# Split projection weights stored once in DRAM scratch and loaded ready in the later rounds

## The chip, the core and the metric

The kernel runs on one core of a Trainium2 chip. The metric is the device time of one execution in microseconds, the median over the runs shown. The core has five engines that run side by side and wait for each other by semaphores: TensorE (PE; its weight loads are shown as PEld), VectorE (DVE), ScalarE (ACT), GpSimd (POOL) and SyncE (SP). SP computes nothing here; it issues nearly all DMAs, strictly in the order of its queue.

## What is computed

One layer of a decoder with two parallel groups of heads, over a prompt of 2048 rows and 8 x 8 sample rows with a paged cache:

```python
h = rmsnorm(x, norm_g)
z = h @ w_in                                   # 1024 -> 3656
q, k, v, qi, ki, wi, ga, u, vm, gm = jnp.split(z, offs, axis=-1)
...
score = indexer_scores(qib, wb, ki)            # causal, 8 index heads
idx, valid = select_keys(score, posb, k_top)   # 256 keys per query
o = sparse_attend(qb, take(k, idx), take(v, idx), valid)
...
mix = concat([attn_o * silu(ga), gelu(u) * s * silu(gm)])
r = x + mix @ w_out
return r + sigmoid(rmsnorm(r, ple_norm_g) @ w_ple_gate) * (p @ w_ple_proj)
```

The case turns on `h @ w_in`, with `w_in` of 1024 x 3656 fp32 values.

## The kernel before

The kernel has three phases. Phase A projects all rows, computes index scores, finds each query's 256 keys and multiplies the gated part by its half of `w_out`. Phase B is attention, phase C the output projection and the gate.

Precision beyond one fp32r matmul is had by splitting: a matrix is written as a high part, rounded to fp32r, and a low part, the rest. `proj` (L290) multiplies high by high, high by low and low by high into one PSUM tile `z`, 24 matmuls for a block of 128 rows and a chunk of columns.

The 17 blocks of rows (16 of the prompt, and SB with the sample rows) are handled in three rounds of 6, 6 and 5 blocks (`ROUNDS`, L55; SB is in the first). In every round all 14 column chunks of `w_in` (`CH`, L57) are loaded again: chunk x1 has 328 columns, the others 256. Chunk x1 holds the index key, x2 the second half of the index queries; then follow vm, k, v, u, gm, q and ga.

`load_w` (L261) fetches a chunk and splits it, in eight steps k of 128 rows. A step loads a raw tile (L270, three buffers), rounds it to the high part `whi` (L275, on POOL; in the very first chunk every other one on ACT, L273) and subtracts to get the low part `wlo` (L276). `WLO_DVE = [6, 5, 0]` says how many of the eight subtractions a round gives to DVE; the rest are POOL's. `whi` and `wlo` have two buffers each. The chunk after the running one is loaded while the running one is multiplied, so its split can start once the last matmul of the chunk before the running one has released the buffer.

After `proj`, `post` (L330) finishes each block: norms, rotary products and activations on ACT, DVE and POOL, and stores of small tiles (`qn`, three buffers; `vt`, two buffers) into DRAM scratch or outputs. `norm_h` (L232) and `split_h` (L246) prepare the rows of the next round during the last chunk of a round: a load of `x` (L226, two buffers), a square on ACT (L241), two small POOL steps (L242, L243), a scaling on DVE (L244), eight transposes on TensorE (L254), and a split on ACT and DVE (L123, L124).

Between the blocks `pump` (L435) advances two other chains: index scores (`idx`, L636: dots on TensorE at L661 and L662, ReLU on ACT at L664, weighted sum on DVE at L666; the sum starts from a ramp that POOL writes at L652) and the search for the 256th score (`topk`, L774: one ACT pass at L802 and a dozen small DVE instructions, seven times, then selections on DVE).

The order on each engine isn't that of the code. The program is built with a scheduler that works from a simulated timeline and places each instruction in its engine's queue. When the instructions change, the order of all engines changes.

Of the kernel before, what the change touches and what calls it, by code (L numbers as in the profile page):

```python
# [9 lines left out]
F32 = mybir.dt.float32  # L10
# [46 lines left out]
CH = [  # L57
    ("x1", [(1536, 72), (1024, 256)]),
    ("x2", [(1280, 256)]),
    ("vm0", [(2632, 256)]),  # L60
    ("vm1", [(2888, 256)]),
    ("k", [(512, 256)]),
    ("v", [(768, 256)]),
    ("u0", [(2120, 256)]),
    ("u1", [(2376, 256)]),
# [45 lines left out]
class Builder:  # L111
# [80 lines left out]
    def phase_a(self, eb):  # L192
        tc, nc, I, O = self.tc, self.nc, self.I, self.O
        with ExitStack() as es:
# [51 lines left out]
            def split_h(b):  # L246
# [3 lines left out]
                for j in range(2):  # L250
# [7 lines left out]
                    else:  # L258
                        self.split(hh[:, s], hl[:, s], ps)

            def load_w(ci, r):  # L261
                name, segs = CH[ci]
                n = sum(s[1] for s in segs)
                wh = wp.tile([128, 8, 328], F32R, name="whi")
                wl = wp.tile([128, 8, 328], F32R, name="wlo")
                for k in range(8):
                    raw = rp.tile([128, 328], F32, name="raw")
                    o = 0
                    for c0, cn in segs:
                        nc.sync.dma_start(raw[:, o:o + cn], I["w_in"][0, k * 128:(k + 1) * 128, c0:c0 + cn])  # L270
                        o += cn
                    if r == 0 and ci == 0 and k % 2:
                        nc.scalar.activation(wh[:, k, :n], raw[:, :n], AF.Copy)  # L273
                    else:
                        nc.gpsimd.tensor_scalar(wh[:, k, :n], raw[:, :n], 1.0, 1.0, op0=OP.mult, op1=OP.mult)  # L275
                    (nc.vector if k < WLO_DVE[r] else nc.gpsimd).tensor_tensor(wl[:, k, :n], raw[:, :n], wh[:, k, :n].bitcast(F32), OP.subtract)  # L276
                return wh, wl, n

            def load_out(j):
# [179 lines left out]
            gb = ac.tile([128, D], F32, name="gb")  # L459
            nc.sync.dma_start(gb, bcast(I["norm_in_g"], D))  # L460
            W0 = load_w(0, 0)
            norm_h(ROUNDS[0][0])
            split_h(ROUNDS[0][0])
# [27 lines left out]
            for si, (r, c) in enumerate(seq):  # L491
                blocks = ROUNDS[r]
                name = CH[c][0]
                nb = ROUNDS[r + 1] if r + 1 < len(ROUNDS) else []
                if name == "vm0":
                    t = vp.tile([128, 6, 512], F32, name="vn")
                    for j, b in enumerate(blocks):
                        vslot[b] = (t, j)
                if si == 1:
                    self.gmlp_weights(ac)  # L500
                nxt = load_w(seq[si + 1][1], seq[si + 1][0]) if si + 1 < len(seq) else None
                if not nxt:
                    ws = [load_out(0)]
# [1045 lines left out]
```

## Time and profile before

| | |
|---|---|
| three runs | 1964.53, 1956.28 and 1952.77 us, median 1956.28 |
| profiled execution, span from the first to the last instruction | 1952.4 us (the page gives no other time for it) |
| TensorE busy | 1865.8 us, 96% |
| DVE, ACT, POOL busy | 67%, 51%, 43% |
| DMA | 202.26 MB, 104 GB/s in the mean |
| HBM | 142.47 MB read, 57.42 MB written |

How to read it. A busy share is the time in which an engine executes at least one instruction; TensorE's matmuls overlap each other, so a busy TensorE is not one at its peak. A wait is idle time of an engine just before an instruction, put down to what released it last. The granted clock of TensorE is a share of its full speed. "DMA share" is the mean busy share of the core's 16 DMA engines. Phase A ends near 1084 us (last matmul of L552), phase B near 1590 us (last of L1128).

### The profile page before, as it was taken

The page shows a single profiled execution, that of the slowest core. Times are in us where ns is not written, and L with a number is a line of the kernel's source. Part 1 is how long each engine was busy: PE and PEld are TensorE (multiplying, and loading weights), DVE is VectorE, ACT ScalarE, POOL GpSimd, SP SyncE. Part 2 cuts the span into 40 slices and gives each one's busy share as a digit, 9 for nine tenths or more (in the row PEclk, how much of TensorE's full clock was granted, in tenths as well). Part 3 has the DMA queues.
Part 4 walks back from the last instruction along what each step waited for, and adds up shares of the span by engine and source line. Part 5 has one row for each costly group of instructions (what it writes and reads, how often), then busy time and mean ns, then how long its engine had stood idle before and what let it go on. Part 6 is the DMA issues. An engine that isn't in the chain of part 4 may idle for free. (4 is left out here: it accounts for less than half of the span.)

```text
span 1952.4 us, 35414 instructions
## 1 busy us (share of the span) xinstructions
PE 1865.8 (96%) x12370; PEld 1655.2 (85%) x12370; DVE 1317.3 (67%) x3682; ACT 995.7 (51%) x1907; POOL 830.4 (43%) x1323
## 2 busy tenths in 40 slices
PE   6989999899999899998999899999999999999998
PEld 5989989897998898997999778887788877888887
DVE  5496566488889758889752688888878865333321
ACT  3234325245555535665664788777867753122211
POOL 5482565554335679547513452213211155222311
PEclk9999999899999999998999999999999999999999
DMA  6423324423333432433455442222222064222311
GB/s 197 112 68 91 113 86 140 125 57 101 85 102 103 144 100 76 126 96 100 135 187 173 142 125 81 81 72 85 64 70 60 27 212 148 90 99 74 116 37 44
DMA packets 193687, 202.26 MB, mean 104 GB/s; under 512 B 85528, under 2 KB 160864, under 8 KB 193376
## 3 DMA queue, kind: packets, MB, share of 16 engines
q1 hardware_dynamic: 187872, 181.08, 30.9%
q0 software_dynamic: 5632, 18.88, 3.1%
q8 instruction: 98, 1.61, 0.4%
q14 instruction: 85, 0.70, 0.1%
HBM read 142.47 MB, written 57.42 MB: 102 GB/s over the span
## 5 line engine op out<-in xcount | busy, mean ns | idle before, releaser
L303 PE MATMUL z<-whi,hhi 128*128 128x256 f32 (+1 forms) x1792 | 461.3, 291 | 14.2 <-ACT qn L376 4.2
L304 PE MATMUL z<-wlo,hhi 128*128 128x256 f32 (+1 forms) x1792 | 455.0, 287 | 2.4 <-POOL wlo L276 2.4
L303 PEld LDWEIGHTS z<-whi,hhi 128*128 128x128 f32 x1792 | 342.7, 191 | 26.7 <-ACT qn L376 6.7
L304 PEld LDWEIGHTS z<-wlo,hhi 128*128 128x128 f32 x1792 | 342.7, 191 | 6.5 <-POOL wlo L276 2.7
L306 PE MATMUL z<-whi,hlo 128*128 128x256 f32 (+1 forms) x1792 | 269.6, 287 | 0.0
L275 POOL TENSOR_SCALAR whi<-raw 128x256 fp32r<-128x256 f32 (+1 forms) x332 | 151.2, 466 | 265.0 <-PE z L306 115.7
L306 PEld LDWEIGHTS z<-whi,hlo 128*128 128x128 f32 x1792 | 240.1, 189 | 4.8
L666 DVE SCALAR_TENSOR_TENSOR big<-dots,sgn,big 128x1024 f32<-128x1024 f32 (+7 forms) x176 | 178.7, 1016 | 43.3 <-ACT dots L664 42.6
L664 ACT ACTIVATE dots<-dots 128x1024 f32<-128x1024 f32 (+7 forms) x176 | 140.5, 801 | 118.4 <-PE dots L662 115.2
L124 DVE TENSOR_TENSOR b_pt<-b_tp,b_pt 128x512 fp32r<-128x512 f32 (+1 forms) x288 | 183.4, 656 | 14.1 <-ACT b_pt L123 12.0
L802 ACT ACTIVATE bfw<-big,tk 128x384 bf16<-128x384 f32 (+14 forms) x105 | 136.6, 1301 | 93.5 <-DVE tk L822 58.7
L123 ACT ACTIVATE b_pt<-b_tp 128x512 fp32r<-128x512 f32 (+1 forms) x288 | 156.1, 579 | 54.2 <-PE b_tp L1111 51.3
L1128 PE MATMUL b_o<-b_pt,Vst 128*128 128x512 f32 x544 | 182.9, 422 | 0.6 <-DVE b_pt L124 0.5
L1085 ACT ACTIVATE b_sm<-b_sm,b_st 128x128 f32<-128x128 f32 (+15 forms) x128 | 155.2, 1214 | 34.7 <-DVE b_st L1078 33.5
L1111 PE MATMUL b_tp<-mats,b_sm 128*128 128x128 f32 x1088 | 171.7, 274 | 0.3 <-ACT b_sm L1085 0.2
L1111 PEld LDWEIGHTS b_tp<-mats,b_sm 128*128 128x128 f32 x1088 | 132.2, 141 | 30.0 <-ACT b_sm L1085 2.0
L276 POOL TENSOR_TENSOR wlo<-raw,whi 128x256 fp32r<-128x256 f32 (+1 forms) x182 | 144.5, 803 | 6.2
L1076 PE MATMUL b_s<-Kst,b_qh 128*128 128x512 f32 (+3 forms) x320 | 139.8, 439 | 6.7 <-DVE b_st L1078 4.8
L1078 DVE CUSTOM_DVE_ANT_0 b_sm<-b_s,b_mask,b_st 128x512 f32<-128x512 f32 (+3 forms) x192 | 124.0, 646 | 23.9 <-PE b_s L1077 19.9
L661 PE MATMUL dots<-ki_stack,qih 128*128 128x512 f32 (+3 forms) x304 | 113.6, 376 | 10.7 <-DVE big L666 10.7
L1077 PE MATMUL b_s<-Kst,b_ql 128*128 128x512 f32 (+3 forms) x320 | 117.9, 371 | 0.1
L662 PE MATMUL dots<-ki_stack,qil 128*128 128x512 f32 (+3 forms) x304 | 111.9, 378 | 0.0
(344 smaller groups left out, 4095.4 us busy)
## 6 DMA issues: line engine op xcount, KB each, us to landing
raw<-w_in SPq DMA_DIRECT2D x336, 128.0 KB
x<-x_prompt SPq DMA_DIRECT2D x16, 512.0 KB
b_qr<-s_q SPq DMA_DIRECT2D x32, 256.0 KB
s_r<-hlo SPq DMA_DIRECT2D x32, 256.0 KB
c_r<-s_r SPq DMA_DIRECT2D x16, 512.0 KB
c_x<-x_prompt SPq DMA_DIRECT2D x16, 512.0 KB
y_prompt<-c_rn SPq DMA_DIRECT2D x15, 512.0 KB
qid<-s_qi SPq DMA_DIRECT2D x56, 128.0 KB
```

Source lines behind the costliest of these rows:

```text
L123: nc.scalar.activation(hi, src, AF.Copy)
L124: nc.vector.tensor_tensor(lo, src, hi.bitcast(F32), OP.subtract)
L275: nc.gpsimd.tensor_scalar(wh[:, k, :n], raw[:, :n], 1.0, 1.0, op0=OP.mult, op1=OP.mult)
L276: (nc.vector if k < WLO_DVE[r] else nc.gpsimd).tensor_tensor(wl[:, k, :n], raw[:, :n], wh[:, k, :n].bitcast(F32), OP.subtract)
L303: nc.tensor.matmul(z, lhsT=hh[:, k], rhs=wh[:, k, :n], start=(k == 0), stop=False)
L304: nc.tensor.matmul(z, lhsT=hh[:, k], rhs=wl[:, k, :n], start=False, stop=False)
L306: nc.tensor.matmul(z, lhsT=hl[:, k], rhs=wh[:, k, :n], start=False, stop=(k == 7))
L664: nc.scalar.activation(r, r, AF.Relu)
L666: nc.vector.scalar_tensor_tensor(a, r, self.sgn[:, b, h:h + 1], a, op0=OP.mult, op1=OP.add)
L1085: nc.scalar.activation(part, part, AF.Exp, bias=stt[:, h, c:c + 1], scale=-1.0, accum_out=stt[:, h, 4 + e:5 + e])
L1111: nc.tensor.transpose(ps[:, k, r], sm2[r][:, (k0 + k) * 128:(k0 + k) * 128 + 128], ident)
L1128: nc.tensor.matmul(o.rearrange("p a b -> p (a b)"), lhsT=Vst[:, kb, g].rearrange("p a d -> p (a d)"), rhs=pt[:, k].rearrange("p a b -> p ( ...
```

## The change

`load_w` gets a second way. Two DRAM scratch tiles per chunk, `s_wh` and `s_wl`, hold the chunk's high and low parts. In round 0 a chunk is loaded and split as before, and then both parts are stored, one DMA each. In rounds 1 and 2 nothing is split: four DMAs bring the two parts, each in two halves of four steps k, straight into `whi` and `wlo`.

```diff
+            kept = [tuple(self.dram.tile([128, 8, sum(s[1] for s in segs)], F32, name=f"s_w{e}{ci}") for e in "hl")
+                    for ci, (_, segs) in enumerate(CH)]
+
             def load_w(ci, r):
                 name, segs = CH[ci]
                 n = sum(s[1] for s in segs)
                 wh = wp.tile([128, 8, 328], F32R, name="whi")
                 wl = wp.tile([128, 8, 328], F32R, name="wlo")
+                halves = tuple(zip((wh, wl), kept[ci]))
+                if r:
+                    for k in range(0, 8, 4):
+                        for t, d in halves:
+                            nc.sync.dma_start(t[:, k:k + 4, :n].bitcast(F32), d[:, k:k + 4])
+                    return wh, wl, n
                 for k in range(8):
...
                     (nc.vector if k < WLO_DVE[r] else nc.gpsimd).tensor_tensor(wl[:, k, :n], raw[:, :n], wh[:, k, :n].bitcast(F32), OP.subtract)
+                for t, d in halves:
+                    nc.sync.dma_start(d, t[:, :, :n].bitcast(F32))
                 return wh, wl, n
```

Lines behind the insertions have numbers that are 9 to 11 higher in the changed kernel (L275 becomes L284, L276 L285, L365 L376); its ready loads stand at L273 and its stores at L287.

The first place is SP's queue at the start, while chunk x1 of round 0 is split. `x` is a block of rows, loaded for blocks 3 and 4 here and at the end for the sample rows; `raw` is a step of weights, `big` a small table. Before:

```order
L226 DMA x_336<-x_prompt 128x1024
L270 DMA raw_440<-w_in 128x256
L609 DMA big_762<-w_s 8x8x8 x6
L226 DMA x_359<-x_prompt 128x1024
L609 DMA big_762<-w_s 8x8x8 x2
L270 DMA raw_444<-w_in 128x256
...
L226 DMA x_382<-x_sample 64x1024
```

And now:

```order
L226 DMA x_366<-x_prompt 128x1024
L279 DMA raw_470<-w_in 128x256
L620 DMA big_794<-w_s 8x8x8 x5
L287 DMA s_wh0_221<-whi_253 128x2624
L226 DMA x_389<-x_prompt 128x1024
L620 DMA big_794<-w_s 8x8x8 x2
L279 DMA raw_474<-w_in 128x256
L620 DMA big_794<-w_s 8x8x8
L287 DMA s_wl0_222<-wlo_254 128x2624
...
L226 DMA x_412<-x_sample 64x1024
```

The store of the high part stands directly ahead of the load of block 4, and that of the low part between it and the load of the sample rows.

The second place is POOL's queue at the step from round 0 to round 1, where the rows of round 1 are normed. `hst` is the statistics tile of a block's norm (L242 and L243), `whi` and `wlo` are the weights of the next chunk, `qn` and `rope_t` a rotary product, `big` the ramp that starts an index sum. Before:

```order
L276 TENSOR_TENSOR wlo_4644<-raw_4665,whi_4643 128x256
L652 TENSOR_SCALAR big_5317<-iota_413 128x768
L242 TENSOR_SCALAR hst_4558<-hst_4558 128x1
L275 TENSOR_SCALAR whi_4643<-raw_4673 128x256
L276 TENSOR_TENSOR wlo_4644<-raw_4669,whi_4643 128x256
L134 TENSOR_TENSOR qn_4712<-qn_4712,ropet_288 128x4x16
L243 TENSOR_TENSOR hst_4558<-hst_4558,half_218 128x1
L276 TENSOR_TENSOR wlo_4644<-raw_4673,whi_4643 128x256
```

And now:

```order
L663 TENSOR_SCALAR big_5253<-iota_443 128x768
L242 TENSOR_SCALAR hst_4516<-hst_4516 128x1
L243 TENSOR_TENSOR hst_4516<-hst_4516,half_218 128x1
L242 TENSOR_SCALAR hst_4578<-hst_4578 128x1
L243 TENSOR_TENSOR hst_4578<-hst_4578,half_218 128x1
L663 TENSOR_SCALAR big_5512<-iota_443 128x896
```

The two steps of one block now stand side by side, and those of the next block follow directly.

The third place is SP's queue in round 1, where chunk x1 is multiplied. `kin` is an index key and `qn` an index query on their way to DRAM. Before, raw loads of chunk vm0 stand between them:

```order
L345 DMA idx_k_prompt<-kin_4927 128x64
L365 DMA s_qi9_77<-qn_4935 128x256
L270 DMA raw_5004<-w_in 128x256
L270 DMA raw_5008<-w_in 128x256
L365 DMA s_qi10_78<-qn_4982 128x256
L345 DMA idx_k_prompt<-kin_4974 128x64
L270 DMA raw_5012<-w_in 128x256
```

And now:

```order
L356 DMA idx_k_prompt<-kin_4919 128x64
L273 DMA wlo_4983<-s_wl2_226 128x4x256
L376 DMA s_qi9_77<-qn_4927 128x256
L273 DMA wlo_4983<-s_wl2_226 128x4x256
L273 DMA whi_4982<-s_wh2_225 128x4x256 x2
L356 DMA idx_k_prompt<-kin_4966 128x64
L376 DMA s_qi10_78<-qn_4974 128x256
```

Four ready loads of 512 KB stand where raw loads of 128 KB stood, and the index queries of blocks 9 and 10 have moved among and behind them.

## Rows read from the trace of the kernel before

**Rows 1.** The page, span and busy time of the engines.

```profile
span 1952.4 us, 35414 instructions
PE 1865.8 (96%) x12370; PEld 1655.2 (85%) x12370; DVE 1317.3 (67%) x3682; ACT 995.7 (51%) x1907; POOL 830.4 (43%) x1323
```

**Rows 2.** Busy time by stretch, rounds 0, 1 and 2; its first line names the columns.

```profile
core 0: us, PE busy (x) PEld busy (x) DVE busy (x) ACT busy (x) POOL busy (x), PEclk, DMA share, GB/s
0.00:324.00 324.00, 298.77 (x2206) 276.23 (x2207) 208.42 (x724) 122.77 (x291) 176.85 (x314) 0.99 0.40 114
324.00:663.00 339.00, 318.58 (x2377) 305.00 (x2378) 267.26 (x867) 166.06 (x316) 166.02 (x294) 0.97 0.36 102
663.00:965.00 302.00, 286.49 (x2062) 269.62 (x2061) 245.70 (x655) 177.11 (x276) 202.36 (x340) 0.98 0.36 104
```

**Rows 3.** Timeline of PE, first matmul of round 1: start us, us, instruction, count.

```profile
323.89 0.39 PE L303 MATMUL z<-whi,hhi 128*128 128x328 f32 x1
```

**Rows 4.** PE's waits in round 1: us in total, times, longest us.

```profile
PE tp L254 <- DVE hlo L124: 6.7, 2, 5.3
PE dots L661 <- DVE big L666: 3.1, 1, 3.1
...
PE tp L322 <- DVE qil L124: 2.3, 1, 2.3
...
PE z L303 <- POOL whi L275: 1.2, 1, 1.2
```

**Rows 5.** PE's waits in round 2.

```profile
PE dots L661 <- DVE big L666: 7.5, 3, 6.8
```

**Rows 6.** POOL's waits in round 0.

```profile
POOL whi L275 <- PE z L296: 46.9, 8, 13.1
```

**Rows 7.** Busy time by stretch, four spots where PE pauses; columns as in rows 2.

```profile
340.00:362.00 22.00, 14.24 (x78) 12.76 (x77) 12.95 (x37) 4.70 (x18) 9.01 (x22) 0.77 0.38 112
436.00:453.00 17.00, 11.61 (x66) 9.32 (x65) 14.94 (x69) 7.42 (x16) 14.75 (x20) 0.85 0.40 113
588.00:613.00 25.00, 20.50 (x140) 18.89 (x139) 24.36 (x74) 11.26 (x19) 15.71 (x24) 0.93 0.28 81
905.00:930.00 25.00, 16.86 (x98) 15.14 (x97) 23.71 (x73) 10.73 (x15) 19.45 (x28) 0.80 0.32 111
```

**Rows 8.** Busy time of L275 alone (POOL), rounds 1 and 2.

```profile
324.00:663.00 339.00, 51.71 (x115) 0.97 0.36 102
663.00:965.00 302.00, 45.74 (x102) 0.98 0.36 104
```

**Rows 9.** Busy time of L276 alone (DVE, then POOL), rounds 1 and 2.

```profile
324.00:663.00 339.00, 31.70 (x65) 39.62 (x47) 0.97 0.36 102
663.00:965.00 302.00, 0.00 (x0) 80.07 (x104) 0.98 0.36 104
```

**Rows 10.** Timeline of POOL at the step from round 0 to round 1.

```profile
336.25 0.19 POOL L242 TENSOR_SCALAR hst<-hst 128x1 f32<-128x1 f32 x1
336.52 1.55 POOL L275 TENSOR_SCALAR whi<-raw 128x256 fp32r<-128x256 f32 x1
338.04 0.73 POOL L276 TENSOR_TENSOR wlo<-raw,whi 128x256 fp32r<-128x256 f32 x1
...
339.02 0.55 POOL L243 TENSOR_TENSOR hst<-hst,half 128x1 f32<-128x1 f32 x1
```

**Rows 11.** Timeline of PE there; in brackets its idle time and the releaser.

```profile
347.79 1.97 PE L254 MATMUL tp<-mats,x 128*128 128x128 f32 x8 [5.28 <-DVE hlo L124]
```

**Rows 12.** Line L132, a rope product on DVE: count, duration ns min/median/max.

```profile
L132 DVE TENSOR_TENSOR rope_t<-qn,ropet x51: 175/185/1864, 128.0 to 935.3; 128x32 f32<-128x32 f32 x48, 64x32 f32<-64x32 f32 x3
```

**Rows 13.** Timeline of POOL in round 2.

```profile
913.04 1.90 POOL L652 TENSOR_SCALAR big<-iota 128x2048 f32<-128x2048 int16 x1
```

**Rows 14.** Timeline of SP at the start, the loads of x for block 4 and the sample.

```profile
24.52 0.36 SPq L226 DMA_DIRECT2D x<-x_prompt  x1
...
35.26 0.48 SPq L226 DMA_DIRECT2D x<-x_sample  x1
```

**Rows 15.** DVE's waits in round 2, the one for a store.

```profile
DVE qn L362 <- DMA s_qi<-qn: 1.5, 1, 1.5
```

## The prediction

> **What bounds the kernel now.** I read the busy shares first: the span is 1952.4 us and TensorE's matmuls are busy for 1865.8 of them, 96% [rows 1]. No other engine comes near, so an instruction taken from VectorE (DVE) or GpSimd (POOL) is worth nothing by itself. It is worth something only where TensorE waits behind it. Second I read the busy times by stage [rows 2]. The three rounds of the projection take 324, 339 and 302 us; a round begins where the 328-wide matmuls of chunk x1 return [rows 3]. In round 1 TensorE is idle 339 - 318.6 = 20.4 us, in round 2 302 - 286.5 = 15.5 us, and the granted clock is 0.97 and 0.98: 3% and 2% short, 10.2 and 6.0 us. The clock has two levels, 1.2 and 2.4 GHz, so these are stretches at the lower one, and the spots below show that they lie at TensorE's pauses. Together 52 us is all that rounds 1 and 2 can give back.
>
> Third I read who ended TensorE's pauses. In round 1 the longest are transposes of the next round's rows behind DVE (6.7 us), index dots behind DVE (3.1) and index queries behind DVE (2.3) [rows 4]; in round 2 index dots behind DVE (7.5) [rows 5]. The weights are hardly a cause: one wait for a high half is there, 1.2 us [rows 4], and GpSimd itself sits idle because the next weight buffer is still being read by matmuls, 46.9 us in eight places of round 0 [rows 6]. Weights come early. Fourth I looked for where the pauses lie: four spots hold 7.8 + 5.4 + 4.5 + 8.1 = 25.8 of the 35.9 idle us, with clocks of 0.77, 0.85, 0.93 and 0.80, which is 5.1 + 2.6 + 1.8 + 5.0 = 14.4 us short [rows 7]. In all four GpSimd is busy for 41 to 87% and DVE for 59 to 97%.
>
> **What goes.** The high halves (L275) take 51.7 us of GpSimd in round 1 and 45.7 in round 2 [rows 8]; the low halves (L276) take 31.7 us of DVE and 39.6 of GpSimd in round 1, and 80.1 of GpSimd in round 2 [rows 9]. All of it goes: 91 and 126 us of GpSimd, 32 us of DVE. It lies beside matmuls, so its direct worth is 0. What it gives at the four spots:
>
> - 340 to 362 us, the step from round 0 to round 1. The rows of the next round go DMA, ScalarE square, two GpSimd steps (L242, L243), DVE scale, TensorE transpose. GpSimd runs L242 at 336.25 and L243 only at 339.02, with a high half of 1.55 us and a low half between [rows 10]; the order shows both gone from there. The two steps take 0.19 and 0.55 us, so 339.02 - 336.44 = 2.6 us of pure queueing goes from one block and some more before L242. TensorE's pause before its last eight transposes is 5.28 us [rows 11]. I take 6 of the 7.8 idle us and 4 of the 5.1 clock us: 10.
> - 436 to 453 us: DVE is busy 14.9 of 17 us, low halves among it. I take 3 of 5.4 idle and 1.3 of 2.6 clock: 4.3.
> - 588 to 613 us: DVE is busy 24.4 of 25 us, mostly with the top-k search, which stays. I take 2 of 6.3.
> - 905 to 930 us, in round 2: no DVE instruction goes there, but GpSimd is busy 19.5 of 25 us. A DVE rope product that takes 185 ns in the median took 1864 ns once [rows 12], at 913 us, while GpSimd ran L652 for 1.90 us beside it [rows 13]. Instructions of the two engines hold each other up, so fewer on GpSimd also shortens DVE's. I take 2.7 of 8.1 idle and 1.7 of 5.0 clock: 4.4.
> - The 10 idle us outside the four spots: 2.
>
> The Trainium skill, page "SBUF — State Buffer", section "SBUF: two separate sides", states that DVE and GpSimd share one pair of ports under an exclusive lock, and the loser waits for the whole instruction. The trace agrees, with 1864 ns beside 1.90 us. Had DVE's instructions kept their length, the 905 us spot would give nothing, and the sum below would be 4.4 us smaller.
>
> Sum of the gains: 10 + 4.3 + 2 + 4.4 + 2 = 22.7, call it 23 us; bounds 0 (the pauses stay) and 52 (all go).
>
> **What comes.** Projection weights are 1024 x 3656 x 4 = 15.0 MB. Round 0 stores both halves, 30 MB more; rounds 1 and 2 read 30 MB in place of 15. The DMA rows give 102 GB/s at a share of 0.36 in round 1 [rows 2], so about 283 GB/s at a full share. A chunk of 2.1 MB then takes 7.4 us by this estimate, and the average chunk lasts 339 / 14 = 24 us and 302 / 14 = 22 us. Shares rise by 53 us of full transfer per later round: 0.36 + 53/339 = 0.52 and 0.36 + 53/302 = 0.54, and in round 0 by 106/324 to 0.73. Three prices:
>
> - The start. The order puts the store of chunk x1's high half ahead of the load of x for block 4, and that of its low half some rows later, ahead of the sample's x. Each is 1.34 MB, 4.7 us by the rate above. In the trace those loads issue at 24.52 and 35.26 us [rows 14]. The store waits for the last high half, whose split ends near 25 us, so block 4 is late by some 5 us; the matmuls of blocks 0 to 3 cover part. Bounds 0 and 9.4; I take 3.
> - The other stores of round 0. SP issues in order, so a store that waits for the splits holds what stands behind it (raw loads, index-query stores). The splits are early (46.9 us above), which is the cover. Were that cover gone, each of 13 chunks could lose a us. Bounds 0 and 13; I take 1.
> - The ready loads. They wait for the weight buffer, which the last matmul of the chunk before frees, so they can start when the running chunk starts, and need 7.4 us of its 22 to 24. SP behind them holds back index-query stores and x loads. I take 1; bounds -3 (SP no longer waits for each split) and 36 (the third rival).
>
> Net: -23 + 3 + 1 + 1 = -18 us. The page gives no time for the profiled execution besides its span of 1952.4, which is 0.4 us below the lowest of the three times and 3.9 below their median of 1956.3. I carry the difference along: 1952.4 - 18 = 1934.4 in span, 1938 as a median.
>
> **Rivals.**
>
> First, the pauses stay where they are. For it: at 588 and 905 us DVE is busy 97% and 95% with the top-k search and index sums, and none of those instructions goes; what TensorE waits for there may be the chain between DVE and ScalarE and not its load. Against it: at 340 us the queueing on GpSimd is plain. Then only the first spot pays, 10, less 5 of costs: -5, so 1951.
>
> Second, DVE and GpSimd free up so much that all four spots go: 25.8 + 14.4 = 40, less 5: -35, so 1921. For it: DVE falls from 267.3 - 31.7 = 235.6 of 339 us in round 1, 70% in place of 79%, before any shortening. Against it: in round 2 DVE stays near 81%.
>
> Third, slower: stores of results stand behind 2.1 MB of ready weights. Eight of the 14 chunks (x1, x2, k, v, q0, q1, ga0, ga1) store a small tile per block; these tiles have two or three buffers, and a block comes every 24 / 6 = 4 us. Two buffers last 8 us, a little more than the 7.4 that a store would be stuck; with SP held on top they run out, and ScalarE, then the two projection banks in PSUM, then TensorE stop. At 1.5 us per such chunk in three rounds that is 24 x 1.5 = 36 us, so -18 + 36 = +18: 1974. It decides from (18 + 19.6) / 24 = 1.6 us per chunk on, when the kernel is over 1% slower. For it: one such wait exists already, DVE for the store of an index query, 1.5 us [rows 15]. Against it: only that one. The Trainium skill, page "DMA: Bandwidth & Descriptors", section "Queues, rings and completion order", states that each DMA engine consumes the descriptors of a queue in ring order, so a small store waits out the whole load ahead; no row here shows more of it than that 1.5 us. A weight load that itself comes late, because SP stood at another wait for over 10 us, belongs here and costs the same way.
>
> **How the numbers follow.** Forecast 0.5, with an own range of 1925 to 1951; pauses stay 0.24; all four go 0.14; slower rival 0.12. About 1% is what a measurement of this kernel can tell from no change, 19.6 us, so faster means under 1936.7 and slower over 1975.8. Faster: 0.14 and nearly half of 0.5, 0.38. Slower: the upper part of the third rival and a little for an order that turns out badly, 0.09. Same: 0.53. The range is 1921 to 1968: from the second rival's price to short of the third's.
>
> **What would show it.** Right: no L275 or L276 from round 1 on; GpSimd near 75 us in each later round (166.0 - 91.3, 202.4 - 125.8), DVE under 236 in round 1; PE idle near 10 us in each; the clock at the first spot up from 0.77; no TensorE wait for a DMA of whi or wlo; round 0 up to 5 us longer. Wrong: rounds 1 and 2 as long as before with idle TensorE at the same spots (first rival), waits of ScalarE or DVE for stores of qn and vt in rows of several us (third), or a round 0 longer by over 10 us.

## The result, and the profile after

The changed kernel takes 1928.01 us (median of four runs, 1925.10 to 1931.14), the kernel before beside it 1955.55 (four runs, 1952.77 to 1964.53). The ratio is 0.985, with a 95% interval of 0.9824 to 0.9876: faster by 1.5%. In the profiled executions the span falls from 1952.4 to 1927.7 us, by 24.7.

The page of the changed kernel, span and busy time, against [rows 1]:

```profile
span 1927.7 us, 34710 instructions
PE 1862.1 (97%) x12370; PEld 1655.8 (86%) x12370; DVE 1252.4 (65%) x3612; ACT 991.1 (51%) x1907; POOL 619.2 (32%) x945
```

GpSimd lost 211 us of work and VectorE 65, and TensorE is as busy as before. Where the 24.7 us came from shows only by stage. Busy time by stretch of the changed kernel, rounds 0, 1 and 2, cut where the 328-wide matmuls of chunk x1 return, against [rows 2]:

```profile
core 0: us, PE busy (x) PEld busy (x) DVE busy (x) ACT busy (x) POOL busy (x), PEclk, DMA share, GB/s
0.00:337.40 337.40, 305.24 (x2213) 280.84 (x2214) 209.34 (x739) 124.50 (x296) 173.21 (x305) 0.95 0.65 203
337.40:652.80 315.40, 312.19 (x2373) 301.38 (x2372) 228.41 (x807) 163.61 (x316) 74.11 (x129) 0.99 0.50 157
652.80:936.20 283.40, 278.82 (x2048) 265.70 (x2047) 210.53 (x606) 165.85 (x264) 84.45 (x134) 0.99 0.51 159
```

In the kernel before, the same cuts lie at 323.8, 662.6 and 964.7 us (rows 2 were rounded to a us). Round 1 is shorter by 23.4 us, round 2 by 18.7, round 0 longer by 13.6, and what follows the rounds by 3.8 (from 964.7 and 936.2 to the ends of the spans, 987.7 and 991.5). So the rounds that load gained 42 us, and 17 were given back. In round 1 TensorE's idle time fell from 20.5 to 3.2 us, in round 2 from 15.5 to 4.6; the rest of the gain is busy time (6.1 and 7.8 us) at a clock that rose from 0.97 and 0.98 to 0.99.

PE's waits in round 1 of the changed kernel: us in total, times, longest us. These are all of them, against [rows 4].

```profile
PE tp L360 <- DVE hlo L124: 1.2, 2, 0.9
PE z L314 <- DVE kin L134: 0.9, 1, 0.9
PE z L314 <- ACT vt L408: 0.6, 1, 0.6
PE tp L254 <- DVE x L244: 0.5, 1, 0.5
```

And in round 2 the wait that answers to [rows 5], 7.5 us there:

```profile
PE dots L672 <- DVE big L677: 0.2, 1, 0.2
```

No wait is for a DMA of `whi` or `wlo`. The four spots of [rows 7] are best compared chunk by chunk, between the same matmuls. First the kernel before: chunk x1 of round 1, its fifth chunk, its eleventh and twelfth, and the twelfth of round 2.

```profile
323.90:361.50 37.60, 29.76 (x181) 28.00 (x182) 25.73 (x79) 13.73 (x38) 18.23 (x39) 0.86 0.41 120
426.00:458.10 32.10, 26.71 (x174) 23.63 (x173) 27.93 (x100) 14.41 (x29) 22.73 (x32) 0.89 0.28 80
571.80:621.50 49.70, 45.20 (x335) 43.05 (x334) 46.77 (x164) 25.75 (x50) 28.94 (x46) 0.97 0.30 89
895.00:927.90 32.90, 24.34 (x149) 22.11 (x149) 31.16 (x94) 16.89 (x26) 26.33 (x37) 0.84 0.33 108
```

The same chunks in the changed kernel:

```profile
337.40:368.40 31.00, 28.43 (x175) 27.43 (x174) 19.14 (x54) 9.88 (x33) 9.67 (x25) 0.89 0.57 178
432.90:456.60 23.70, 23.63 (x175) 21.77 (x174) 20.57 (x90) 12.20 (x27) 14.45 (x20) 1.00 0.53 161
570.70:614.50 43.80, 43.80 (x338) 42.46 (x337) 40.75 (x150) 23.82 (x48) 17.24 (x24) 1.00 0.46 149
879.40:898.50 19.10, 18.86 (x142) 17.88 (x141) 15.40 (x53) 13.04 (x22) 9.30 (x12) 1.00 0.44 140
```

They give 6.6, 8.4, 5.9 and 13.8 us, 34.7 of the 42. In the last three TensorE has hardly a gap left and the full clock. The DVE column goes along with it: in the fifth chunk DVE had been busy for 27.9 of 32.1 us, now for 20.6 of 23.7, with 10 instructions fewer (five of them low halves, 3.9 us); in the chunk of round 2, where no instruction of the splits was DVE's, 53 instructions stand where 94 did, fewer rope products and less of the search. What made the chunks shorter isn't told by this column alone; that is for the experiments.

Round 0 pays in two places. Busy time by stretch, its first chunk, the ten next, and the last three; before, then after:

```profile
0.00:52.70 52.70, 34.45 (x188) 31.61 (x189) 30.71 (x81) 18.98 (x48) 25.91 (x57) 0.97 0.64 191
52.70:264.50 211.80, 205.17 (x1565) 190.44 (x1564) 141.09 (x511) 79.00 (x185) 119.17 (x205) 0.99 0.34 95
264.50:323.90 59.40, 59.05 (x457) 54.08 (x456) 36.51 (x132) 24.68 (x58) 31.68 (x53) 1.00 0.41 117
```

```profile
0.00:58.00 58.00, 36.36 (x189) 33.81 (x190) 31.23 (x81) 19.02 (x48) 25.64 (x57) 0.82 0.82 258
58.00:269.50 211.50, 207.08 (x1565) 190.55 (x1564) 138.58 (x499) 76.74 (x184) 118.94 (x201) 0.98 0.63 193
269.50:337.40 67.90, 61.79 (x462) 56.48 (x463) 39.52 (x159) 28.74 (x65) 28.63 (x49) 0.97 0.57 187
```

The start costs 5.3 us (matmuls begin at 11 us in both), the ten chunks nothing, the last three 8.5. In these three ScalarE waits for its small stores, which it didn't before; ACT's waits there in the changed kernel:

```profile
ACT qn L387 <- DMA s_q<-qn: 3.9, 1, 3.9
...
ACT vt L408 <- DMA s_ga<-vt: 3.7, 1, 3.7
```

TensorE's two longest pauses in the same stretch stand behind just these two instructions:

```profile
PE z L314 <- ACT vt L408: 2.8, 2, 2.5
PE z L307 <- ACT qn L387: 2.3, 1, 2.3
```

### The profile page after: what moved, and what is told of

It is laid out like the page before. It is cut to its first block, busy times and chain, and to the rows that moved or that the text cites. A ratio compares the mean times of both kernels' runs of the same rounds, so it can differ in the third digit from the quotient of the medians.

```text
span 1927.7 us, 34710 instructions
## 1 busy us (share of the span) xinstructions
PE 1862.1 (97%) x12370; PEld 1655.8 (86%) x12370; DVE 1252.4 (65%) x3612; ACT 991.1 (51%) x1907; POOL 619.2 (32%) x945
## 5 line engine op out<-in xcount | busy, mean ns | idle before, releaser
L1444 PE MATMUL c_mm<-c_l_w_ple_gate,c_mh 128*128 128x512 f32 x272 | 106.9, 393 | 2.6 <-DVE c_l_w_ple_gate L1397 2.6
L1443 PE MATMUL c_mm<-c_h_w_ple_gate,c_mh 128*128 128x512 f32 x272 | 109.0, 401 | 0.0
```

Source lines behind the costliest of these rows:

```text
L1443: nc.tensor.matmul(z, lhsT=hi[:, k], rhs=wts[k][0][:, ns], start=(k == 0), stop=False)
L1444: nc.tensor.matmul(z, lhsT=hi[:, k], rhs=wts[k][1][:, ns], start=False, stop=(b == SB and k == nk - 1))
```

## The experiments

Two questions were open: what gives the 42 us back in rounds 1 and 2, and what makes round 0 longer. Every run is compared with the kernel before on the same chip. The stages are those of the profiled executions, cut as above; "rest" is the span from the end of round 2 on, in which all these kernels have the same code. A stage is known from one execution of each kernel, the median from all of them.

| | median us | ratio to before, 95% | round 0 | round 1 | round 2 | rest |
|---|---|---|---|---|---|---|
| before | 1955.6 | | 323.8 | 338.8 | 302.1 | 987.7 |
| the change | 1928.0 | 0.982 to 0.988 | 337.4 | 315.4 | 283.4 | 991.5 |
| e1 idle work, both | 1981.6 | 1.010 to 1.024 | 336.4 | 362.5 | 281.5 | 997.9 |
| e2 idle work, GpSimd | 1975.2 | 1.007 to 1.017 | 345.7 | 359.5 | 278.4 | 987.9 |
| e3 idle work, DVE | 1932.1 | 0.983 to 0.989 | 339.2 | 323.2 | 277.7 | 995.9 |
| e4 two chunks stored | 1916.0 | 0.977 to 0.981 | 329.6 | 313.4 | 282.5 | 985.5 |
| e5 paced, GpSimd reads | 1979.9 | 1.010 to 1.015 | 336.8 | 326.3 | 309.5 | 1002.4 |
| e6 paced, GpSimd writes | 1945.1 | 0.993 to 0.996 | 339.3 | 331.3 | 285.6 | 993.6 |
| e7 stores from ScalarE | 1924.6 | 0.982 to 0.985 | 340.1 | 312.5 | 282.7 | 993.2 |
| e8 stores from GpSimd | 1927.9 | 0.984 to 0.987 | 339.5 | 311.5 | 283.5 | 990.6 |
| e9 x1 stored later | 1928.1 | 0.982 to 0.987 | 342.2 | 313.0 | 282.3 | 988.8 |
| e10 last three stored later | 1933.2 | 0.985 to 0.990 | 329.6 | 325.6 | 281.2 | 995.7 |
| e11 both stored later | 1932.9 | 0.984 to 0.989 | 337.7 | 327.6 | 277.8 | 989.1 |
| e12 stores in pieces | 1918.3 | 0.978 to 0.983 | 332.3 | 312.8 | 282.9 | 988.5 |

"Rest" runs from 985.5 to 1002.4 us with the same code; the 3.8 us by which the change is longer there are inside that scatter, and I don't explain them.

**The work given back: e1 to e3.** The removed passes are put back as idle ones, on a constant, into raw tiles that nobody reads. e2:

```diff
                             nc.sync.dma_start(t[:, k:k + 4, :n].bitcast(F32), d[:, k:k + 4])
+                    for k in range(8):
+                        dp = rp.tile([128, 328], F32, name="raw")[:, :n]
+                        nc.gpsimd.tensor_scalar(dp, gb[:, 0:n], 1.0, 1.0, op0=OP.mult, op1=OP.mult)
+                        if k >= WLO_DVE[r]:
+                            nc.gpsimd.tensor_tensor(dp, gb[:, 0:n], gb[:, 328:328 + n], OP.subtract)
```

e3 has DVE's five subtractions of round 1 instead, e1 both.

> Ready loads as in the changed kernel, but in rounds 1 and 2 GpSimd and VectorE get as many instructions of the same kinds and sizes as the splits had (8 roundings and 3 or 8 subtractions on GpSimd, 5 or 0 on VectorE per chunk), on constants, with results that nobody reads. Engine theory (the gain is the load taken from GpSimd and VectorE): rounds 1 and 2 together go from 599 us back to about 640, so 1958 to 1970 us. Rival A (the gain is the DMA side: fewer raw loads, SP no longer held by the splits): nothing changes there, 1926 to 1933. Rival B (a luckier order of the scheduler): anywhere, with idle TensorE not where the engines are busy.

> Only GpSimd's part of the idle work comes back (8 roundings and 3 or 8 subtractions per chunk in rounds 1 and 2). Engine theory: most of the gain goes, since GpSimd lost 217 us and VectorE 32: 1943 to 1958 us, with VectorE's instructions lengthened again in both rounds. If VectorE's own 32 us were the cause: 1928 to 1934. Rival A: 1926 to 1933.

> Only VectorE's part comes back: 5 subtractions per chunk in round 1, none in round 2. Engine theory: round 1 longer by 3 to 12 us, round 2 unchanged, 1931 to 1940 us. If VectorE's own load were the main cause: round 1 back to near 339, 1945 to 1952. Rival A: 1926 to 1933.

e3 costs 7.8 us in round 1 and 4 in the time, as expected. e1 and e2 are slower than the kernel before and 12 and 17 us above their ranges, but not in the way expected: round 2 stays at 278 to 282 us. The stretches of e2 show the reason:

```profile
345.70:705.20 359.50, 323.88 (x2385) 309.31 (x2383) 284.64 (x840) 172.83 (x328) 253.42 (x462) 0.94 0.44 139
705.20:983.60 278.40, 276.18 (x2045) 263.70 (x2043) 208.06 (x584) 161.81 (x258) 80.95 (x133) 1.00 0.51 162
```

GpSimd is busy for 253 us in round 1 and 81 in round 2. The idle work reads a constant and waits for nothing, and the scheduler ran it early: round 1 had most of both shares (the changed kernel has 74 us there), round 0 a little, round 2 none. For the question the accident is a good control. The ready loads are the same in both rounds; the round with GpSimd's passes is long, the one without stays short. So ready loads alone don't make a round short; how much the passes cost at their own pace is not told by these runs.

**At the pace of the chunks: e5 and e6.** e5's idle passes read the loaded chunk, so they wait for it as the splits did. e6 reads 8 columns for the pace and then only writes.

```diff
+                        # e5
+                        nc.gpsimd.tensor_scalar(dp, wh[:, k, :n].bitcast(F32), 1.0, 1.0, op0=OP.mult, op1=OP.mult)
+                        if k >= WLO_DVE[r]:
+                            nc.gpsimd.tensor_tensor(dp, wh[:, k, :n].bitcast(F32), wl[:, k, :n].bitcast(F32), OP.subtract)
+                        # e6
+                        nc.gpsimd.tensor_scalar(dp[:, 0:8], wh[:, k, 0:8].bitcast(F32), 1.0, 1.0, op0=OP.mult, op1=OP.mult)
+                        for i in range(2 if k >= WLO_DVE[r] else 1):
+                            nc.gpsimd.memset(dp, 1.0)
```

> The changed kernel, in which GpSimd also reads each loaded chunk in rounds 1 and 2 as it read it to split it: 8 passes over the high part and 8 (from row WLO_DVE on) subtractions of the low part, into the raw tiles that nobody reads. The results are as before; the work waits for the loaded chunk, so that it can't run rounds ahead as in the runs e1 and e2. Theory (the gain is the GpSimd's time given back): both rounds lose, round 1 from 315 to about 335 us, round 2 from 283 to about 300, VectorE's lengthening returns in both, time 1950 to 1968 us. Rival (the gain is in the loads: no raw tiles on SP's queue): the two rounds stay at 315 and 283 us, time 1926 to 1934 us.

> The same place and pace as e5, but GpSimd only writes: of each row it reads 8 columns of the loaded chunk and then fills the raw tile with a constant, once or twice where e5 has one or two passes. The results are as before. Theory A (what costs is that GpSimd is occupied, so its other work comes later): as e5, in proportion to the time the fills take. Theory B (what costs is that GpSimd's passes lengthen VectorE's operations beside them): with nothing read there is less to share, VectorE's lengthening stays near 13 and 11 us as in the changed kernel, and the time is 1928 to 1938 us.

Rounds 1 and 2 of e5, then of e6:

```profile
336.80:663.10 326.30, 315.05 (x2368) 303.13 (x2368) 238.87 (x819) 166.59 (x319) 150.55 (x286) 0.98 0.48 152
663.10:972.60 309.50, 287.67 (x2045) 268.68 (x2044) 230.39 (x593) 160.56 (x259) 205.31 (x346) 0.98 0.47 146
```

```profile
339.30:670.60 331.30, 318.23 (x2376) 304.95 (x2375) 233.45 (x829) 170.61 (x325) 136.35 (x403) 0.98 0.47 150
670.60:956.20 285.60, 279.07 (x2044) 264.46 (x2043) 206.75 (x587) 160.00 (x256) 152.04 (x443) 1.00 0.50 159
```

In e5 both rounds lose, 10.9 and 26.1 us, with no byte more to load. So GpSimd's time carries the gain, as the theory said (the time, 1979.9, is 12 above its range, and the rest is 11 us longer than in the change): in round 2 it carries more than the 18.7 us gained, in round 1 10.9 of 23.4. As it takes more than was gained, e5's passes don't cost quite what the splits did. In round 2, where DVE has no work of the splits in either kernel, reading and writing part: 121 us of GpSimd passes that read cost 26.1, 68 us of fills 2.2, so 0.22 against 0.03 us for each. (The fills are also shorter instructions, 316 ns in the mean against 445 and 778; no run tells length from reading.) e6's time, 1945.1, lies 7 us above the range of theory B, by its round 1. How DVE fares beside them shows in its instructions with both inputs in SBUF. Two groups of DVE's instructions in round 2 (busy us, mean ns of one | idle before and its releaser), first in the kernel before:

```profile
L424 DVE TENSOR_TENSOR vn<-vn,vt 128x256 f32<-128x256 f32 x20 | 10.9, 547 | 0.2 <-ACT vt L421 0.2
...
L132 DVE TENSOR_TENSOR rope_t<-qn,ropet 128x32 f32<-128x32 f32 x15 | 6.6, 440 | 0.1
```

In the changed kernel:

```profile
L435 DVE TENSOR_TENSOR vn<-vn,vt 128x256 f32<-128x256 f32 x20 | 8.3, 416 | 0.7 <-ACT vt L432 0.7
...
L132 DVE TENSOR_TENSOR rope_t<-qn,ropet 128x32 f32<-128x32 f32 x15 | 4.0, 265 | 0.1
```

In e5:

```profile
L440 DVE TENSOR_TENSOR vn<-vn,vt 128x256 f32<-128x256 f32 x20 | 10.4, 520 | 0.7 <-ACT vt L437 0.7
...
L132 DVE TENSOR_TENSOR rope_t<-qn,ropet 128x32 f32<-128x32 f32 x15 | 5.1, 343 | 0.1
```

In e6:

```profile
L440 DVE TENSOR_TENSOR vn<-vn,vt 128x256 f32<-128x256 f32 x20 | 8.7, 434 | 0.7 <-ACT vt L437 0.7
...
L132 DVE TENSOR_TENSOR rope_t<-qn,ropet 128x32 f32<-128x32 f32 x15 | 3.3, 221 | 0.1
```

The same 20 instructions take 547, 416, 520 and 434 ns in the mean, the same 15 take 440, 265, 343 and 221: longer by a quarter to two thirds beside GpSimd passes that read, hardly or not beside those that write. The means hide how it happens. Of the 20, 13 take 409 to 421 ns in the kernel before, as all 20 do in the changed kernel (411 to 425), and seven take 501 to 1254; the median doesn't move. So some instructions are held up for long, and the others not at all. Nor does every group follow: the last step of the rope product (L135, also two inputs in SBUF) takes 253 ns in the kernel before and 336 in the changed one. The weighted sum, whose dots come from PSUM, doesn't change with any of it; in the changed kernel it takes 1281 ns, in the one before 1275:

```profile
L677 DVE SCALAR_TENSOR_TENSOR big<-dots,sgn,big 128x1024 f32<-128x1024 f32 x43 | 55.1, 1281 | 22.7 <-ACT dots L675 22.5
```

The Trainium skill, page "SBUF — State Buffer", section "Who interferes with whom", states that a DVE instruction with two SBUF inputs contends with a GpSimd instruction that reads SBUF and not with one that only writes it. The means of these two groups agree, that of L135 doesn't.

In round 1 it isn't so clean. The rope product's mean follows (227, 184, 285 and 185 ns), that of the `vn` group doesn't (432, 458, 465 and 419), and the fills cost 15.9 us, more than the reading passes with 10.9. There is a sign of a second mechanism, GpSimd's queue: in e6 the six searches of the round together stand 11.2 us at their starts (4.8 at most) until GpSimd comes to a small step of them (L800), in round 1 of the changed kernel 0.4. This group of e6, then that of the changed kernel:

```profile
L807 DVE SCALAR_TENSOR_TENSOR tk<-guess,tk 128x1 f32<-128x1 f32 x6 | 1.3, 219 | 11.2 <-POOL tk L800 11.2
```

```profile
L802 DVE SCALAR_TENSOR_TENSOR tk<-guess,tk 128x1 f32<-128x1 f32 x6 | 1.3, 216 | 0.6 <-POOL tk L795 0.4
```

In the kernel before it was 0.2, so this wait is the fills' own; that it reaches TensorE isn't shown. What share of round 1's 23.4 us came from longer instructions, from the queue and from DVE's own subtractions stays open. e5 and e3 put back 10.9 and 7.8 us there, 18.7 together, but in two runs. So the work of the splits, and not the loads, is shown to be the cause for round 2 and for most of round 1.

**Round 0, how much of it the stores are: e4.** Only chunks x1 and x2 are stored; the later rounds load x2's parts for all other chunks.

```diff
-                halves = tuple(zip((wh, wl), kept[ci]))
+                halves = tuple(zip((wh, wl), kept[min(ci, 1)]))
-                            nc.sync.dma_start(t[:, k:k + 4, :n].bitcast(F32), d[:, k:k + 4])
+                            nc.sync.dma_start(t[:, k:k + 4, :n].bitcast(F32), d[:, k:k + 4, :n])
-                for t, d in halves:
-                    nc.sync.dma_start(d, t[:, :, :n].bitcast(F32))
+                if ci < 2:
+                    for t, d in halves:
+                        nc.sync.dma_start(d, t[:, :, :n].bitcast(F32))
```

> Only chunks x1 and x2 are stored in round 0; in rounds 1 and 2 all other chunks load x2's parts, so that their products are of other weights (the index scores stay as they are). The loads keep number and size. Store theory (round 0 lost 13 us to the stores, about 5 at its start and 8 later): round 0 shorter by 6 to 10 us, 1918 to 1923 us. If round 0 lost to its order or its start alone: 1926 to 1930.

Round 0 falls by 7.8 us to 329.6, nearly all of it in the last three chunks (60.2 us from 67.9; before 59.4). The start stays 5 us longer than before. Rounds 1 and 2 are as in the change. So the stores of twelve chunks cost 8 us, and only at the end of the round. (The time, 1916.0, is 2 us below the store theory's range.)

**Another queue: e7 and e8.** The stores leave SP's queue, so that nothing stands behind them in it.

```diff
-                    nc.sync.dma_start(d, t[:, :, :n].bitcast(F32))
+                    nc.scalar.dma_start(d, t[:, :, :n].bitcast(F32))     # e7; nc.gpsimd in e8
```

> The changed kernel with the two stores of each chunk in round 0 issued by ScalarE instead of SyncE, so that SP's queue holds none of them. Theory (round 0 is longer because small transfers stand behind the stores on SP's queue): x of block 4 and of the sample come as early as before, the waits of ScalarE for s_q and s_ga in chunks 11 to 13 go, round 0 is 324 to 330 us and the time 1914 to 1922 us. Rival (round 0 is longer because the 16.8 MB of stores share the DMA engines and DRAM with everything else): round 0 stays at 335 to 340 us, time 1926 to 1932 us. A second cost to watch: ScalarE waits in its own order until the low half is there.

> The same as e7 with GpSimd as the issuer, which makes the high half and most of the low one itself, and so waits least for them. Theory (place in SP's queue): round 0 is 324 to 330 us, time 1914 to 1922 us, unless the issue on GpSimd takes over 2 us each (32 of them, then up to 10 us of round 0 come back through GpSimd, which is busy 217 of 324 us there). Rival (the bytes): round 0 stays at 335 to 340 us, time 1926 to 1932 us.

Round 0 stays at 340 us in both: the theory of the place in SP's queue falls in this form. (e7's time, 1924.6, lies between the two ranges, e8's in the rival's. The stores of round 0 are 30.0 MB and not 16.8, and 28 and not 32; GpSimd is busy for 173 us there in the changed kernel and not 217.) In e7 the wait for `s_q` in the last three chunks shrinks from 3.9 to 2.4 us, but ScalarE now stands in its own order until GpSimd has made the parts; ACT's waits in the last three chunks of e7:

```profile
ACT sq L382 <- POOL whi L284: 5.1, 1, 5.1
```

In e8 nobody waits in that way, and yet the store of `qn`, on SP's queue without the big stores, is late:

```profile
ACT qn L387 <- DMA s_q<-qn: 5.1, 2, 4.5
```

So in e8 small transfers are late beside 1 MB stores that stand in another queue. The Trainium skill, page "DMA: Bandwidth & Descriptors", section "Queues, rings and completion order", states that each DMA engine takes turns between its queues, one packet at a time; the 4.5 us agree with a small store that shares the engines with a large one.

**Storing some chunks a round later: e9 to e11.** The named chunks are split once more in round 1, stored there, and loaded ready in round 2 alone. e9 does so with x1, e10 with q1, ga0 and ga1, e11 with all four.

```diff
-                if r:
+                first = 1 if ci in (0,) else 0        # e10: (11, 12, 13); e11: (0, 11, 12, 13)
+                if r > first:
...
-                for t, d in halves:
-                    nc.sync.dma_start(d, t[:, :, :n].bitcast(F32))
+                if r == first:
+                    for t, d in halves:
+                        nc.sync.dma_start(d, t[:, :, :n].bitcast(F32))
```

> The changed kernel, but the first chunk (x1) isn't stored in round 0: it is split again in round 1, stored there, and loaded ready in round 2 alone. The results are as before. Theory (the first chunk's stores are what makes round 0's start longer): chunk x1 is back at 42 us from 47, round 0 at 331 to 333 us, round 1 longer by 1 to 3 us for one chunk's split, time 1922 to 1928 us. Rival (the start is longer for another reason, a clock that falls lower there with no store in flight): chunk x1 stays at 46 to 47 us and the time is 1927 to 1932 us.

> The changed kernel, but the last three chunks (q1, ga0, ga1) aren't stored in round 0: split again in round 1, stored there, loaded ready in round 2 alone. The results are as before. Theory (their stores and those just ahead of them make chunks 11 to 13 longer by 8.5 us, whichever queue holds them): the three chunks are back at 59 to 61 us from 68, round 0 at 328 to 331 us, round 1 longer by 3 to 6 us, time 1922 to 1928 us. Rival (it is the loads of round 1 that come into the end of round 0, not the stores): the three chunks stay at 65 us or more, time 1930 to 1935 us.

> Both at once: x1, q1, ga0 and ga1 are stored in round 1 and not in round 0. The results are as before. If both costs of round 0 are those of these chunks' stores and add up, round 0 is 323 to 327 us, round 1 320 to 325 us (from 315), round 2 283 us, time 1918 to 1926 us. If stores elsewhere or other reasons hold them, round 0 stays above 331 us and the time at or over 1928 us.

e10 settles the end of round 0: with these three chunks' stores gone they take 60.3 us, TensorE is busy for 59.8 of them at the full clock, and round 0 is back at 329.6.

```profile
269.30:329.60 60.30, 59.76 (x465) 54.90 (x463) 37.81 (x154) 28.20 (x63) 27.30 (x46) 1.00 0.44 141
```

It doesn't pay, because three chunks split in round 1 cost 10.2 us there (315.4 to 325.6; 3 to 6 were expected), with 18 us more of GpSimd (92.07 against 74.11) and 10 more of DVE. This is the price of the splits once more, from the other side.

e9 and e11 were to settle the start, and don't. In e9 chunk x1 takes 43.6 us in round 0, in e11, with no store of it either, 46.5; the change has 46.8, the kernel before 41.6. The theory that its own stores make the start longer fails on e11, the rival (43.6) on e9. But length alone misleads, as these chunks differ in what makes them long. From its first matmul to the end of the chunk TensorE idles for 9.1 us in the kernel before, 12.4 in the change, 11.9 in e9 and 9.6 in e11, and is busy for 32.5, 34.5, 31.7 and 36.9. So the change loses 3.4 us to pauses and 1.9 to longer matmuls (up to the end of that chunk its clock was 0.82, before it was 0.97), e9 loses to pauses alone (0.94), e11 nearly to the clock alone (0.85). TensorE's first long pause for scaled rows, 3.06 us (1.46 before), ends at 23.86 us, ahead of the first store at 25.34, so no store makes it. A second one, 3.66 us, is absent in the kernel before. It stands behind the scaling of the sample rows, which takes 2.73 us on DVE (1.28 before, in e9 and in e11) while GpSimd runs splits of the next chunk beside it:

```profile
43.71 2.73 DVE L244 SCALAR_TENSOR_TENSOR x<-x,hst,gb 64x1024 f32<-64x1024 f32 x1
43.96 1.40 POOL L285 TENSOR_TENSOR wlo<-raw,whi 128x256 fp32r<-128x256 f32 x2
46.59 0.42 PE L254 MATMUL tp<-mats,x 64*128 64x64 f32 x2 [3.66 <-DVE x L244]
```

That is again an instruction with two inputs in SBUF beside GpSimd's. Whether x1's stores bring the two together isn't shown (in e10, with the same stores at the start, this pause is 0.84 us), so the start stays open. Both runs also lose the end of round 0 again (71.3 and 64.7 us for the last three chunks). x1's split for round 1 now falls there; TensorE's waits in the very last chunk are for ScalarE's `vt` (3.9 us in e9, 2.2 in e11) and of the next rows' transposes for DVE (3.7 and 1.9). How much of it the split brings isn't told.

**Small pieces: e12.** The stores are held back and spread. Each chunk's parts go in eight pieces, one behind every row that is loaded of the next chunk.

```diff
+            held = []
+            def keep(m):
+                for t, d in held[:m]:
+                    nc.sync.dma_start(d, t.bitcast(F32))
+                del held[:m]
...
                 if r:
+                    keep(8)
...
                         o += cn
+                    keep(1)
...
-                for t, d in halves:
-                    nc.sync.dma_start(d, t[:, :, :n].bitcast(F32))
+                held.extend((t[:, k:k + 2, :n], d[:, k:k + 2]) for k in range(0, 8, 2) for t, d in halves)
```

> The changed kernel, but in round 0 a chunk's parts aren't stored in two transfers of 1.3 MB: eight pieces of two rows each are held back and one is issued behind each row's load of the next chunk, all chunks stored in the end. The results are as before, and the bytes the same. Theory (a small transfer is late because it stands behind 2.6 MB of stores issued at once, on its own queue or beside it on the shared DMA engines): the waits of ScalarE for s_q and s_ga in chunks 11 to 13 go or fall under 1.5 us each, these chunks take 60 to 63 us instead of 68, round 0 is 327 to 332 us, rounds 1 and 2 stay at 315 and 283, time 1918 to 1923 us. Rival (it is the sum of the bytes beside the rest, whenever they move): round 0 stays at 335 to 340 us, time 1926 to 1932 us.

It is as the theory has it, but for the three chunks, which take 63.9 us, a little over the forecast 63. Stretches of e12, rounds 0 to 2 and the last three chunks of round 0:

```profile
0.00:332.30 332.30, 304.03 (x2214) 280.39 (x2214) 208.67 (x739) 124.83 (x296) 170.50 (x305) 0.97 0.68 206
332.30:645.10 312.80, 310.63 (x2372) 300.06 (x2371) 228.93 (x808) 163.72 (x316) 74.26 (x129) 0.99 0.50 158
645.10:928.00 282.90, 278.25 (x2047) 265.28 (x2046) 210.53 (x603) 165.72 (x264) 84.28 (x134) 0.99 0.50 159
268.40:332.30 63.90, 61.63 (x466) 56.62 (x464) 37.95 (x152) 28.10 (x63) 25.15 (x44) 0.97 0.62 197
```

ScalarE's wait for `s_q` there is gone, and of that for `s_ga` this is left:

```profile
ACT vt L416 <- DMA s_ga<-vt: 1.2, 1, 1.2
```

The same bytes move, and DMA is even a little busier (0.68 against 0.65 in round 0). Their grain is another, and the moment of each piece with it, so the sum of the bytes is not the cost. e12 is the fastest kernel with the full result: 1918.25 us (1914.63 to 1923.09), 1.9% under the kernel before; its interval and that of the change just touch.

## Why the prediction was right, and where it was wrong

The forecast was 18 us less in span, it became 24.7; 1928 lies 10 us under the forecast of 1938 and inside the range. The direction holds, and the cause does for round 2 and most of round 1. "Within 1%", to which I gave the most, did not come true: the upper end of the interval is 1.2% faster. And the sum is near partly by luck: two terms were too small, one on each side.

- **The gain, 23 forecast, 42 measured.** The mechanism (GpSimd's passes delay its own steps and lengthen DVE's instructions) holds by e5 and e6, the lengthening in round 2 above all. Its size was missed at the spots where I took part of the pause for DVE's own search. By chunk the spots gave 6.6 (forecast 10), 8.4 (4.3), 5.9 (2) and 13.8 (4.4); elsewhere rounds 1 and 2 gave 7.4 (2). The failed step is "which stays": I counted which DVE instructions go, and priced the lengthening of the others by a single outlier of 1864 ns [rows 12], where seven of the 20 `vn` products of round 2 were held up (mean 547 ns, without the splits 416). Three of the four spots have the full clock now, 1.00; at the first, where I took most, the chunk's clock rose only from 0.86 to 0.89.
- **The second rival** was nearest for rounds 1 and 2: it put the four spots at 40; they gave 34.7, the two rounds 42. Its time, 1921, is 7 us from the measured one, mine 10. It had only 0.14, because round 2's DVE share was to stay near 81%. It fell to 74% (210.53 of 283.4) with no instruction of the splits gone from DVE there; part of that is shorter instructions, part work that now stands in other stages (606 instructions for 655).
- **The start, 3 forecast (0 to 9.4), 5.3 measured.** The size is inside the bounds, the reason given (stores ahead of x) isn't shown: the first longer pause ends before any store is issued, the second goes with a scaling that took 2.73 us for 1.28, and e11 has a long start without that store, by its clock.
- **The other stores of round 0, 1 forecast (0 to 13), 8.5 measured.** The step that failed is the cover: the early splits hide SP's wait for them, but not the transfers. ScalarE's small stores are late beside the 1 MB stores, and it waits for the buffers of `qn` and `vt`. e4, e10 and e12 show it. The text named a round 0 longer by over 10 us as a sign against it; it is longer by 13.6.
- **The third rival's mechanism is real, in another place.** I looked for small stores stuck behind ready loads, 24 times in three rounds, though only two rounds have such loads (16 times). It happened behind the stores of round 0, in three chunks, for 8.5 us. In rounds 1 and 2 ScalarE and DVE have a few such waits (4.5 us for `s_q`, 7.0 for `s_qi`), but none reaches TensorE.
- **The ready loads, 1 forecast.** Nothing of a loss is seen: e2 runs round 2 in 278.4 us with the same loads. Shares of 0.50 and 0.51 were forecast at 0.52 and 0.54, and 0.73 in round 0 came out at 0.65.
- GpSimd near 75 us per later round came in round 1 (74.1), in round 2 it was 84.5; DVE under 236 in round 1 (228.4) came as the text said; TensorE's idle time, forecast near 10 us each, fell to 3.2 and 4.6.

## What to carry to other kernels

An engine that is off the critical path can still set the length of its neighbour's instructions: before costing its removed work at nothing, compare the means of DVE forms with two SBUF inputs, and not their medians, between a stage where GpSimd reads much and one where it is idle. Work stored once for later rounds did better here in small pieces between the loads than in one transfer of a MB at the moment it was ready, whichever queue that stood in. An idle-work experiment should wait for the same data as the work it stands for, or a scheduler may move it into another stage, as here.

## What was not expected of the hardware

That GpSimd's passes hold up so many of DVE's two-input instructions, and not one or two: in round 2 the rope product took 440 ns in the mean beside the splits and 265 without, its median in the whole kernel before being 185 [rows 12], and seven of 20 `vn` products were held up. And ScalarE waited 4.5 us for a small store on SP's queue beside 1 MB stores that had been issued from another queue (e8).
